# Hybrid encoder step on one core: stick-breaking attention written as a sum over running products times differences of neighbouring values

## The chip, the cores and the metric

The kernel runs on one core of one Trainium2 chip. The metric is the time of one execution in microseconds of the device. Before the change the median of three runs was 3561.26 us (3555.72 to 3566.15). Engines are named as in the profile: PE (TensorE matmul), PEld (its weight load), DVE (VectorE), ACT (ScalarE), POOL (GpSimd), SP (SyncE, which here only issues DMAs).

## The reference, cut to what matters

One layer: a norm, one wide projection, two mixers (stick-breaking attention with 8 heads of 64, and an RWKV recurrence with 8 heads), an output projection and a gated feed-forward layer, for a prompt of 2048 rows and a sample of 32 rows with 1024 cached keys. The change is in the attention of the prompt:

```python
z = jnp.einsum('bqhd,bkhd->bhqk', q, k) / math.sqrt(SB_HEAD_DIM)
mask = k_pos[None, :] < q_pos[:, None]
log_1mb = jnp.where(mask, jax.nn.log_sigmoid(-z), 0.0)
after = lax.cumsum(log_1mb, axis=3, reverse=True) - log_1mb
weight = jnp.where(mask, jnp.exp(jax.nn.log_sigmoid(z) + after), 0.0)
o = jnp.einsum('bhqk,bkhd->bqhd', weight, v)
```

So the weight of key s is sigmoid(z_s) times the product over all later keys j of (1 - sigmoid(z_j)). With R_s the product of sigmoid(-z_j) over all j from s on, that weight is R_(s+1) - R_s.

## The kernel before, in words

The program has three stages, and a scheduler that writes out one fixed order of instructions for each engine.

**Projection** (to about 911 us of the profiled execution). Three blocks of the prompt (5, 6 and 5 tiles of 128 rows); for each, 27 column groups of the projection in turn, each by three rounds of 8 matmuls (L323). The group of the attention's values is `g_va`, four times in each block: the columns are copied from PSUM to `vq`, and a deferred `fin` turns them on PE into rows (`tok_major`, L307, PSUM pool `psT` with 3 buffers), stores these, and splits them into a high and a low part `vs` (L656 on ACT, L657 on DVE) that are stored as `vhl_d`. `vs` lies in the tag `hl6`, of which there is one buffer; `qhl` of `g_qk` uses the same.

**Attention, recurrence and the first half of the output projection** (911 to about 1905 us). Three generators are interleaved by weights: `attention`, `recurrence` and `first_rows` (L738, `mo`). The attention goes over heads twice: first all 8 heads with the query groups 0 and 1 (512 queries each), here called the first half, then all 8 with the groups 2 and 3, the second half. For each group it goes down the key pieces `kc` of 512 keys, and for each piece over four tiles `j` of 128 queries; one such `scores` is a step. There are 96 steps in the first half (12 a head) and 224 in the second (28 a head); between heads 1 and 2 of the first half lies the sample's attention (6 steps). On the diagonal (`kc == qg`) a step has (j+1)*128 keys, else 512.

A step: two matmuls give `z` (L794, L795; PSUM pool `psZ`, 3 buffers), a third adds the mask on the diagonal (L797); `stick` then takes sigmoid(-z) to `R` (L754) and sigmoid(z) to `b` (L755) on ACT, DVE turns `R` into running products from the right (L757, a scan whose two operands are both `R`), and POOL multiplies `b` by the `R` of the next key (L758). Four steps later at the earliest `turn` transposes `b` on PE into `wt` (L809, `psW`, 2 buffers), and ACT and DVE split it into `wth` and `wtl` (L103, L104); two steps later `values` multiplies both parts with the values (L823, L824). `k` and `vp` are loaded at the first step that needs them (5 buffers each), `q` likewise.

**Feed-forward** (from about 2015 us): PE alone, L1268 and L1288.

Of the kernel before, what the change touches and what calls it, by code (L numbers as in the profile page):

```python
# [9 lines left out]
F32 = mybir.dt.float32  # L10
# [37 lines left out]
def f32(ap):  # L48
    return ap.bitcast(F32)
# [3 lines left out]
def kernel(ctx: ExitStack, tc: tile.TileContext, x_prompt, x_sample, cache_k, cache_v,  # L53
# [17 lines left out]
    vhl_d = [dp.tile([TP, 2, P], F32, name=f"vhl_d{c}") for c in range(4)]  # L71
    QR_d = dp.tile([NCH + 1, 4, P, P], F32, name="QR_d")
# [40 lines left out]
    with tc.tile_pool(name="pa0", bufs=1) as pe, tc.tile_pool(name="pa1", bufs=1) as pa, \  # L113
# [37 lines left out]
        R_MU, R_ST, R_W0, R_A0, R_KK, R_KA, R_RK = 0, 15, 30, 34, 38, 42, 46  # L151
# [110 lines left out]
        def superblock(sb, T0, NTILE):  # L262
# [478 lines left out]
    with tc.tile_pool(reuse_waits="tile", name="bp", bufs=6) as bp, \  # L741
# [8 lines left out]
        NB, LAG, LAG2, RW = 10, 4, 2, PAST + TS + 1  # L750

        def stick(z, R, b, k0, n):

# [8 lines left out]
        def queue(h):  # L762

            return ACT if h == 0 else SP

        def load(h, kc):
            k = bp.tile([P, 512], F32R, tag="k", name="k", bufs=5)
            queue(h).dma_start(f32(k), khl_d[h // 2][h % 2].rearrange("l d t -> (l d) t")[:, kc * 512:(kc + 1) * 512])
            v = bp.tile([P, 4, P], F32R, tag="vp", name="vp", bufs=5)
            queue(h).dma_start(f32(v), vhl_d[h // 2][kc * 512:(kc + 1) * 512, h % 2, :].rearrange("(j p) e -> p j e", p=P))  # L770
            pieces[h, kc] = [k, v]

        def scores(h, qg, kc, j):

            if kc == qg and j == 0:
                q = bp.tile([P, 2, 512], F32R, tag="q", name="q", bufs=3)
                cs = slice(qg * 512, (qg + 1) * 512)
                queue(h).dma_start(f32(q[:, 0]), qhl_d[h // 2][h % 2].rearrange("l d t -> (l d) t")[:, cs])
                for l in range(2):
                    queue(h).dma_start(f32(q[64 - 64 * l:128 - 64 * l, 1]), qhl_d[h // 2][h % 2, l, :, cs])  # L780
                state[h, qg] = q
            if j == 0 and (kc == qg or (qg == 2 and kc < 2)):
                load(h, kc)
            if kc == qg:
                R = bk.tile([P, RW], F32, tag="R", name="R")
                e = (qg % 2) * 512 + (j + 1) * P
                POOL.memset(R[:, e:e + 1], 1.0)
                state[h, qg, "R", j] = R
            R = state[h, qg, "R", j]
# [12 lines left out]
            state[h, qg, kc, j] = b  # L802
# [13 lines left out]
        def values(h, qg, kc, kb):  # L816
# [6 lines left out]
            PE.matmul(av[:, c0:], v[:, kb, :], wh[:, c0:], start=kc == qg and kb == 0, stop=False)  # L823
            PE.matmul(av[:, c0:], v[:, kb, :], wl[:, c0:], start=False, stop=kc == 0 and kb == 3)  # L824
# [7 lines left out]
        def s_scores(kc, e):  # L832
            n = TS if kc == 2 else 512
            if kc == 2:
                R = bk.tile([P, RW], F32, tag="R", name="Rs")
# [20 lines left out]
            b = bk.tile([P, 512], F32, tag="b", name="bs", bufs=NB)  # L856
            stick(z, state["R", e], b, kc * 512, n)
# [36 lines left out]
        def attention():  # L894
            A, B = [], []
            for hq, h in [(hq, h) for hq in range(2) for h in range(H)]:
# [7 lines left out]
                for qg in (2 * hq, 2 * hq + 1):  # L904
                    for kc in range(qg, -1, -1):
                        for j in range(4):
                            n = (j + 1) * P if kc == qg else 512
                            A.append((lambda h=h, qg=qg, kc=kc, j=j: scores(h, qg, kc, j), 2 * n / 2400))
# [446 lines left out]
```

## Time and profile before

| | |
|---|---|
| median of three runs | 3561.26 us |
| profiled execution, its time | 3553.88 us |
| its span, first to last instruction | 3551.9 us |
| PE, DVE, ACT, POOL busy over the span | 94%, 53%, 36%, 37% |
| granted TensorE clock, mean | 0.959 |

The span is 2 us shorter than the execution's time. A busy share is an average over the three stages, of which only the middle one is touched deeply by the change; it is read by stages below. A PE that is busy is not a PE at its peak, since the profile counts each matmul to its modelled end.

### The profile page before, as it was taken

To read this page: it belongs to the slowest core of one execution; us is meant where nothing else is said; L and a number is where in the kernel's file an instruction comes from. 1 tells how busy PE (TensorE), PEld (TensorE's weight loads), DVE (VectorE), ACT (ScalarE), POOL (GpSimd) and SP (SyncE) were. 2 spreads that over 40 slices of the span, in tenths; PEclk is the share of its full clock that TensorE was granted. 3 is DMA by queue.
4 is the path that set the end of the run, shared out by engine and by line. 5 is a ranking of instruction groups with operands and counts; after the bars stand their busy time and mean duration, and the time that the engine had idled before them with its cause. 6 is when DMAs were issued, how large, how long until landed. Compare 5 with 4: busy or idle time off the path is not lost.

```text
span 3551.9 us, 51561 instructions
## 1 busy us (share of the span) xinstructions
PE 3348.1 (94%) x20217; PEld 2888.5 (81%) x20217; DVE 1875.3 (53%) x2437; ACT 1265.8 (36%) x2419; POOL 1299.2 (37%) x1207
## 2 busy tenths in 40 slices
PE   8999999989788889998998999999999999999998
PEld 7988898879566677776777899989998888888887
DVE  4665757668876788988884332232222412212213
ACT  6444343443444566665563321111111311111111
POOL 3322433243444576657664322211221222122121
PEclk9999999999787899998999999999999999999999
DMA  5545655566644555554554341111111511111111
GB/s 150 162 145 152 201 147 151 181 172 182 198 117 114 133 148 142 150 139 127 154 138 137 118 132 48 48 36 48 48 48 36 167 60 48 48 48 48 48 42 48
DMA packets 480362, 395.81 MB, mean 111 GB/s; under 512 B 70820, under 2 KB 402160, under 8 KB 480120
## 3 DMA queue, kind: packets, MB, share of 16 engines
q1 hardware_dynamic: 391672, 346.51, 34.1%
q10 hardware_dynamic: 88448, 46.01, 4.8%
q8 instruction: 159, 2.61, 0.3%
q14 instruction: 83, 0.68, 0.1%
HBM read 278.16 MB, written 114.28 MB: 110 GB/s over the span
## 4 chain that ended last, share of the span: by engine, by line
PE 74%; DVE 14%; issue 4%; POOL 3%; ACT 2%; DMA 2%; SPq 0%; ACTq 0%; POOLq 0%; DVEq 0%
PE gu L1268 28%; PE dn L1288 14%; PE mm L323 12%; DVE R L757 5%; PE mo L738 4%; PE wt L809 2%; DVE wtl L104 2%; DVE t L541 1%; DVE Ti L543 1%; PE av L823 1%; PE a4ps L504 1%; PE av L824 1%; PE z L794 1%; PE sap L1067 1%; PE snp L1076 1%
## 5 line engine op out<-in xcount | busy, mean ns | idle before, releaser
L758 POOL TENSOR_TENSOR b<-b,R 128x512 f32<-128x512 f32 (+2 forms) x320 | 394.4, 1238 | 271.9 <-DVE R L757 174.1
L757 DVE TENSOR_TENSOR_SCAN R<-R 128x512 f32<-128x512 f32 (+2 forms) x320 | 440.9, 1387 | 40.0 <-ACT R L754 36.8
L1291 DVE TENSOR_TENSOR x<-x,dn 128x512 f32<-128x512 f32 x374 | 255.6, 687 | 243.4 <-PE dn L1288 243.4
L1268 PE MATMUL gu<-h2h,wh 128*128 128x352 f32 (+1 forms) x1760 | 368.3, 351 | 1.7 <-ACT wh L103 1.2
L1268 PE MATMUL gu<-h2h,wl 128*128 128x352 f32 (+1 forms) x1760 | 369.0, 351 | 0.0
L1268 PE MATMUL gu<-h2l,wh 128*128 128x352 f32 (+1 forms) x1760 | 367.3, 351 | 0.0
L1268 PEld LDWEIGHTS gu<-h2h,wh 128*128 128x128 f32 x1760 | 305.0, 188 | 33.9 <-ACT wh L103 1.4
L1268 PEld LDWEIGHTS gu<-h2l,wh 128*128 128x128 f32 x1760 | 305.3, 188 | 31.0
L1268 PEld LDWEIGHTS gu<-h2h,wl 128*128 128x128 f32 x1760 | 305.1, 188 | 30.2
L1288 PE MATMUL dn<-dh,hdh 128*128 128x512 f32 x748 | 295.1, 394 | 0.0
L1288 PE MATMUL dn<-dh,hdl 128*128 128x512 f32 x748 | 295.0, 394 | 0.0
L1288 PE MATMUL dn<-dl,hdh 128*128 128x512 f32 x748 | 293.8, 393 | 0.0
L809 PE MATMUL wt<-ident,b 128*128 128x128 f32 x1088 | 203.6, 300 | 87.5 <-DVE wtl L104 67.5
L809 PEld LDWEIGHTS wt<-ident,b 128*128 128x128 f32 x1088 | 137.2, 150 | 144.1 <-DVE wtl L104 68.9
L323 PE MATMUL mm<-hh,wh 128*128 128x384 f32 (+4 forms) x1296 | 248.2, 335 | 5.8 <-DVE qhl L614 2.0
L323 PE MATMUL mm<-hh,wl 128*128 128x384 f32 (+4 forms) x1296 | 234.6, 324 | 0.0
L323 PE MATMUL mm<-hl,wh 128*128 128x384 f32 (+4 forms) x1296 | 231.9, 321 | 0.0
L754 ACT ACTIVATE R<-z 128x512 f32<-128x512 f32 (+2 forms) x320 | 174.5, 545 | 142.3 <-PE z L795 69.2
L323 PEld LDWEIGHTS mm<-hh,wh 128*128 128x128 f32 (+1 forms) x1296 | 212.7, 194 | 13.1 <-DVE qhl L614 2.3
L103 ACT CAST wth<-wt 128x512 fp32r<-128x512 f32 (+1 forms) x320 | 169.7, 533 | 135.2 <-PE wt L809 124.7
L323 PEld LDWEIGHTS mm<-hh,wl 128*128 128x128 f32 (+1 forms) x1296 | 211.2, 190 | 2.6
L104 DVE TENSOR_TENSOR wtl<-wt,wth 128x512 fp32r<-128x512 f32 (+1 forms) x320 | 188.7, 595 | 41.3 <-ACT wth L103 38.4
(752 smaller groups left out, 5899.3 us busy)
## 6 DMA issues: line engine op xcount, KB each, us to landing
wraw<-in_w_in ACTq DMA_DIRECT2D x77, 512.0 KB
rawg<-in_w_gate SPq DMA_DIRECT2D x44, 512.0 KB
rawu<-in_w_up SPq DMA_DIRECT2D x44, 512.0 KB
rawd<-in_w_down SPq DMA_DIRECT2D x44, 512.0 KB
A_d<-a SPq DMA_DIRECT2D x28, 512.0 KB
mx<-mixT_d SPq DMA_DIRECT2D x27, 512.0 KB
k<-khl_d SPq DMA_DIRECT2D x42, 256.0 KB
vp<-vhl_d SPq DMA_DIRECT2D x42, 256.0 KB
```

Source lines behind the costliest of these rows:

```text
L103: ACT.copy(hi, src)
L104: (eng or DVE).tensor_tensor(lo, src, f32(hi), ALU.subtract)
L323: PE.matmul(ps[0:wd, 0:s1 - s0], a_[:, kt, 0:wd], b_[:, kt, s0:s1], start=i == 0, stop=i == 3 * KT - 1)
L504: PE.matmul(ps[:, j, :], KB[64 * e:64 * e + 64, j0 + j, :], QR[64 * e:64 * e + 64, j0 + j, :], start=True, stop=True)
L738: PE.matmul(ps[0:n], a_[:, kt, 0:n], b_[:, kt, :], start=j + kt == 0, stop=j == 2 and kt == KT - 1)
L754: ACT.activation(R[:, k0:k0 + n], z[:, 0:n], AF.Sigmoid, scale=-0.125)
L757: DVE.tensor_tensor_scan(rv, rv, rv, R[:, k0 + n:k0 + n + 1], ALU.mult, ALU.bypass)
L758: POOL.tensor_tensor(b[:, 0:n], b[:, 0:n], R[:, k0 + 1:k0 + n + 1], ALU.mult)
L809: PE.transpose(pt[:, j * P:(j + 1) * P], state[h, qg, kc, j][:, kb * P:(kb + 1) * P], ident)
L1268: PE.matmul(ps[:, 0:n], a_[:, kt, :], b_[:, kt, s0:s1], start=i == 0, stop=i == 23)
L1288: PE.matmul(ps[0:n], a_[:, i * P:i * P + n], b_[:, ds_], start=k == 0, stop=k == 3 * len(js) - 1)
L1291: DVE.tensor_tensor(x1[:n, ds_], x1[:n, ds_], ps[0:n], ALU.add)
```

## The change

It leaves `b` out. The sum over s of (R_(s+1) - R_s) v_s is summed by parts, to a sum of R_s (v_(s-1) - v_s). The differences `dv` are made in the projection (two subtractions on POOL for each `g_va`, the last column of the block before kept in spare columns of `cols`), transposed on PE (`pdv`), split into `vs` and stored as `vhl_d` in place of the values. On the diagonal, where R is 1 from the query on, the last row of each tile of 128 keys has to be v_(s-1) alone: these rows are stored as `ve_d`, and a diagonal block loads a second copy of its values, `vd`, with that row replaced. `values` on the diagonal therefore takes `vd` for the 128 queries of the tile, and `vp` for those after it: four matmuls instead of two, of as many columns together.

`stick` is one sigmoid and one scan. The scan's second operand, which the operation BYPASS ignores, is now `z` in PSUM instead of `R` in SBUF, and it starts from the first column of the piece to the right. `R` is a tile of its own for each step (12 buffers) and goes into `turn` in place of `b`. The sample's attention keeps the old form (`s_stick`). `load` is called up to 8 steps before the first step that needs it (`LOOK`), with 6 buffers for `k` and `vp`.

```diff
@@ g_va
+                dv = pr.tile([P, 2, MX], F32, tag="hl6", name="dv", bufs=1)[:, 0]
+                pv_ = cols[:, R_PV + c:R_PV + c + 1]
+                POOL.tensor_tensor(dv[:, 0:1], pv_, vq[:, 0:1], ALU.subtract)
+                POOL.tensor_tensor(dv[:, 1:NP], vq[:, 0:NP - 1], vq[:, 1:NP], ALU.subtract)
+                ACT.copy(pv_, vq[:, NP - 1:NP])
...
-                    vs = pr.tile([P, 6, 2, P], F32R, tag="hl6", name="vs", bufs=1)
-                    v4 = vt[:, 0:NTILE, :].rearrange("p j (h d) -> p j h d", d=HD)
-                    ACT.copy(vs[:, 0:NTILE, :, 0:64], v4)
-                    DVE.tensor_tensor(vs[:, 0:NTILE, :, 64:128], v4, f32(vs[:, 0:NTILE, :, 0:64]), ALU.subtract)
-                    SP.dma_start(vhl_d[c][T0:T0 + NP].rearrange("(j t) h e -> t j h e", t=P),
-                                 f32(vs[:, 0:NTILE]))
+                    for q0 in range(0, NTILE, 4):
+                        pt = psT.tile([P, 4, P], F32, tag="tr", name="pdv")
+                        m = min(q0 + 4, NTILE) - q0
+                        for i in range(m):
+                            PE.transpose(pt[:, i, :], dv[:, (q0 + i) * P:(q0 + i + 1) * P], ident)
+                        vs = r4("vs").bitcast(F32R).rearrange("p (j h e) -> p j h e", j=4, h=2)
+                        split(vs[:, 0:m, :, 0:64], vs[:, 0:m, :, 64:128],
+                              pt[:, 0:m, :].rearrange("p j (h d) -> p j h d", d=HD))
+                        t0 = T0 + q0 * P
+                        SP.dma_start(vhl_d[c][t0:t0 + m * P].rearrange("(j t) h e -> t j h e", t=P), f32(vs[:, 0:m]))
+
+                    pe_ = psT.tile([P, 512], F32, tag="tr", name="pve")
+                    PE.transpose(pe_[0:NTILE, 0:P], vq[:, 0:NP].rearrange("p (j t) -> p j t", t=P)[:, :, P - 2], ident)
+                    ve = pr.tile([P, 256], F32, tag="t2", name="ve").bitcast(F32R).rearrange("p (h e) -> p h e", h=2)
...
+                    SP.dma_start(ve_d[c, T0 // P:T0 // P + NTILE], f32(ve[0:NTILE]))
@@ attention
-        NB, LAG, LAG2, RW = 10, 4, 2, PAST + TS + 1
+        NB, LAG, LAG2, LOOK, RW = 12, 4, 2, 8, PAST + TS + 1
+        def stick(z, R, n, before):
+
+            ACT.activation(R[:, 0:n], z[:, 0:n], AF.Sigmoid, scale=-0.125)
+            rv = R[:, 0:n][:, ::-1]
+            DVE.tensor_tensor_scan(rv, rv, z[:, 0:n], before, ALU.mult, ALU.bypass)
...
+            k = bp.tile([P, 512], F32R, tag="k", name="k", bufs=6)
...
+            v = bp.tile([P, 4, P], F32R, tag="vp", name="vp", bufs=6)
+            dma(f32(v), src)
             if kc == qg:
...
+                vd = bp.tile([P, 4, P], F32R, tag="vd", name="vd", bufs=3)
+                dma(f32(vd[0:P - 1]), src[0:P - 1])
+                dma(f32(vd[P - 1:P]), ve_d[h // 2, 4 * qg:4 * qg + 4, h % 2, :].unsqueeze(0))
...
-            b = bk.tile([P, 512], F32, tag="b", name="b", bufs=NB)
-            if kc % 2 and kc < qg:
-                POOL.tensor_copy(R[:, 1024:1025], R[:, 0:1])
-            stick(z, R, b, (kc % 2) * 512, n)
+            R = bk.tile([P, 512], F32, tag="R", name="R", bufs=NB)
+            stick(z, R, n, 1.0 if kc == qg else state[h, qg, kc + 1, j][:, 0:1])
...
-            PE.matmul(av[:, c0:], v[:, kb, :], wh[:, c0:], start=kc == qg and kb == 0, stop=False)
-            PE.matmul(av[:, c0:], v[:, kb, :], wl[:, c0:], start=False, stop=kc == 0 and kb == 3)
+            if kc == qg:
+                vd = state[h, qg, "vd"]
+                for i, w_ in enumerate((wh, wl)):
+                    PE.matmul(av[:, c0:c0 + P], vd[:, kb, :], w_[:, c0:c0 + P], start=kb + i == 0,
+                              stop=qg == 0 and kb == 3 and i == 1)
+                c0 += P
+            if c0 < 512:
+                PE.matmul(av[:, c0:], v[:, kb, :], wh[:, c0:], start=False, stop=False)
+                PE.matmul(av[:, c0:], v[:, kb, :], wl[:, c0:], start=False, stop=kc == 0 and kb == 3)
...
+                while loads and loads[0][0] <= t + LOOK:
+                    load(*loads.pop(0)[1:])
```

The scheduler's order also moves. On PE, where one head of the first half ends and the next begins (between its 60th and 61st `z`, heads 4 and 5), there stood before, from the last `z` of the one head to the first of the next:

```order
L794 MATMUL z<-k,q 128x512
L795 MATMUL z<-k,q 128x512
L823 MATMUL av<-wth,vp 128x256
L809 MATMUL wt<-ident,b 128x128 x4
L824 MATMUL av<-wtl,vp 128x256
L823 MATMUL av<-wth,vp 128x128
L809 MATMUL wt<-ident,b 128x128 x3
...
L823 MATMUL av<-wth,vp 128x512
L824 MATMUL av<-wtl,vp 128x512
L794 MATMUL z<-k,q 128x128
```

The rows left out are more `wt`, `av` and rows of the recurrence; eight whole `turn`s stand between the two `z`. In the changed kernel the same place reads, on PE:

```order
L822 MATMUL z<-k,q 128x512
L823 MATMUL z<-k,q 128x512
L852 MATMUL av<-wth,vd 128x128
L852 MATMUL av<-wtl,vd 128x128
L856 MATMUL av<-wth,vp 128x384
L857 MATMUL av<-wtl,vp 128x384
...
L852 MATMUL av<-wth,vd 128x128
L822 MATMUL z<-k,q 128x128
L835 MATMUL wt<-ident,R 128x128 x4
L852 MATMUL av<-wtl,vd 128x128
```

The next head's first `z` now stands ahead of the first of those turns, and one turn then follows each `z`. At all seven boundaries between heads of the first half, five to nine turns stood between two `z`; in the changed kernel so many stand there at the sample's place (eight) and twice around the last head (five and eight), and elsewhere at most four.

The other place is on ACT, where the projection ends and the attention begins. Before, the loads of head 0 (ACT's queue issues them) stood among the last copies of the projection, the first of them 25 rows ahead of the first sigmoid:

```order
L778 DMA q<-qhl_d_57 128x512
L642 COPY vq<-mm 128x256
L780 DMA q<-qhl_d_57 64x512 x2
L768 DMA k<-khl_d_61 128x512
L770 DMA vp<-vhl_d_65 128x4x128
```

Now they stand behind all of it, on ACT, one after the other, right ahead of the first sigmoid:

```order
L104 CAST vs<-pdv 128x2x64
L796 DMA q<-qhl_d_57 128x512
L104 CAST ve<-pve 5x2x64
L798 DMA q<-qhl_d_57 64x512 x2
L803 DMA k<-khl_d_61 128x512
L808 DMA vp<-vhl_d_65 128x4x128
L812 DMA vd<-vhl_d_65 127x4x128
L813 DMA vd<-ve_d 1x4x128
...
L813 DMA vd<-ve_d 1x4x128
L772 ACT_TABLE_LOAD
L772 ACTIVATE R<-z 128x128
```

The rows left out are the same seven loads for the second query group: 14 issues in all, ten before.

## Rows read from the trace of the kernel before

**Rows 1.** The page: span and instructions; shares of the chain that ended last.

```profile
span 3551.9 us, 51561 instructions
PE 74%; DVE 14%; issue 4%; POOL 3%; ACT 2%; DMA 2%; SPq 0%; ACTq 0%; POOLq 0%; DVEq 0%
```

**Rows 2.** Both halves: PE, PEld, DVE, ACT, POOL busy; clock, DMA share, GB/s.

```profile
911.00:1206.00 295.00, 238.24 (x1648) 187.31 (x1649) 211.99 (x284) 146.47 (x337) 151.90 (x181) 0.77 0.50 132
1206.00:1878.00 672.00, 612.50 (x5065) 488.25 (x5065) 582.73 (x636) 407.04 (x818) 453.65 (x453) 0.95 0.53 140
```

**Rows 3.** Waits in the second half: total us, times, longest us.

```profile
POOL b L758 <- DVE R L757: 119.4, 86, 5.4
PEld wt L809 <- DVE wtl L104: 46.0, 37, 3.8
PE wt L809 <- DVE wtl L104: 42.9, 39, 3.7
```

**Rows 4.** Windows, matmuls of L794 alone, in six stretches of the first half.

```profile
962.00:987.00 25.00, 0.00 (x0) 0.00 (x0) 0.86 0.57 171
...
1098.00:1115.00 17.00, 0.00 (x0) 0.00 (x0) 0.70 0.44 122
1134.00:1151.00 17.00, 0.00 (x0) 0.00 (x0) 0.70 0.28 77
1167.00:1190.00 23.00, 0.00 (x0) 0.00 (x0) 0.55 0.44 127
sum 120.00, PE 0.00 PEld 0.00; mean PE 0.00 PEld 0.00
```

**Rows 5.** Windows, scans of L757 alone (DVE busy), first and second half.

```profile
911.00:1206.00 295.00, 117.97 (x100) 0.77 0.50 132
1206.00:1878.00 672.00, 327.30 (x225) 0.95 0.53 140
```

**Rows 6.** Groups by shape, 935 to 1910 us: busy us, mean ns.

```profile
L757 DVE TENSOR_TENSOR_SCAN R<-R 128x512 f32<-128x512 f32 x221 | 353.1, 1603 | 21.4 <-ACT R L754 19.3 <-POOL R L800 0.3
L104 DVE TENSOR_TENSOR wtl<-wt,wth 128x512 fp32r<-128x512 f32 x223 | 150.0, 677 | 35.2 <-ACT wth L103 33.1
L1083 DVE TENSOR_TENSOR VST<-VST,PC 64x512 f32<-64x512 f32 x31 | 35.7, 1151 | 1.0
L758 POOL TENSOR_TENSOR b<-b,R 128x512 f32<-128x512 f32 x223 | 294.6, 1326 | 176.5 <-DVE R L757 116.2 <-ACT b L755 17.7 <-ACT R L754 11.8
```

**Rows 7.** Timeline of DVE at the attention's first scans: start us, us.

```profile
921.30 0.47 DVE L757 TENSOR_TENSOR_SCAN R<-R 128x128 f32<-128x128 f32 x1
...
921.87 0.74 DVE L757 TENSOR_TENSOR_SCAN R<-R 128x256 f32<-128x256 f32 x1
...
922.69 1.01 DVE L757 TENSOR_TENSOR_SCAN R<-R 128x384 f32<-128x384 f32 x1
...
924.22 1.27 DVE L757 TENSOR_TENSOR_SCAN R<-R 128x512 f32<-128x512 f32 x1
```

**Rows 8.** Timeline, one step of the second half: matmul, sigmoid of `b`, scan.

```profile
1402.52 0.39 PE L795 MATMUL z<-k,q 128*128 128x512 f32 x1
...
1403.44 0.59 ACT L755 ACTIVATE b<-z 128x512 f32<-128x512 f32 x1
...
1403.77 1.26 DVE L757 TENSOR_TENSOR_SCAN R<-R 128x512 f32<-128x512 f32 x1
```

**Rows 9.** Timeline of the weight loads of two 128-column matmuls of `values`.

```profile
1408.07 0.19 PEld L823 LDWEIGHTS av<-wth,vp 128*128 128x128 f32 x1
...
1408.18 0.19 PEld L824 LDWEIGHTS av<-wtl,vp 128*128 128x128 f32 x1
```

**Rows 10.** The chain in order of time: one run of 512-column matmuls.

```profile
2085.86 24.97 PE dn L1288 x108
```

**Rows 11.** Timeline of PE in the projection: the transposes of one `tok_major`.

```profile
866.21 0.77 PE L307 MATMUL ptok<-ident,vq 128*128 128x128 f32 x5
```

**Rows 12.** Groups of POOL in the projection: busy us, mean ns.

```profile
L344 POOL TENSOR_TENSOR df<-xp 128x673 f32<-128x673 f32 (+5 forms) x45 | 65.4, 1453 | 196.3 <-ACT xp L335 123.6 <-ACT xp L337 50.4 <-ACT bon L486 18.2
```

**Rows 13.** Tile `q`: ACT's own issues of its loads, min/median/max ns.

```profile
L780 ACTq DMA_DIRECT2D q<-qhl_d x8: 452/603/978, 876.9 to 1247.1; - x8
```

**Rows 14.** Timeline of ACT at the first sigmoid.

```profile
917.58 0.28 ACT L754 ACTIVATE R<-z 128x128 f32<-128x128 f32 x1
```

More of the change, by code (lines that the diff above doesn't have):

```diff
@@ L71 @@
     vhl_d = [dp.tile([TP, 2, P], F32, name=f"vhl_d{c}") for c in range(4)]
+    ve_d = dp.tile([4, TP // P, 2, P], F32, name="ve_d")
     QR_d = dp.tile([NCH + 1, 4, P, P], F32, name="QR_d")
@@ L653, in fin @@
                         SP.dma_start(sv[:, c * P:(c + 1) * P], vt[0:TS, NTILE, :])
-                    vs = pr.tile([P, 6, 2, P], F32R, tag="hl6", name="vs", bufs=1)
-                    v4 = vt[:, 0:NTILE, :].rearrange("p j (h d) -> p j h d", d=HD)
-                    ACT.copy(vs[:, 0:NTILE, :, 0:64], v4)
-                    DVE.tensor_tensor(vs[:, 0:NTILE, :, 64:128], v4, f32(vs[:, 0:NTILE, :, 0:64]), ALU.subtract)
-                    SP.dma_start(vhl_d[c][T0:T0 + NP].rearrange("(j t) h e -> t j h e", t=P),
-                                 f32(vs[:, 0:NTILE]))
+                    for q0 in range(0, NTILE, 4):
[11 more added lines that the diff above has]
+                    ve = pr.tile([P, 256], F32, tag="t2", name="ve").bitcast(F32R).rearrange("p (h e) -> p h e", h=2)
+                    split(ve[0:NTILE, :, 0:64], ve[0:NTILE, :, 64:128],
+                          pe_[0:NTILE, 0:P].rearrange("p (h d) -> p h d", d=HD))
+                    SP.dma_start(ve_d[c, T0 // P:T0 // P + NTILE], f32(ve[0:NTILE]))
                 defer(1, fin)
@@ L764, in queue, with load @@
             return ACT if h == 0 else SP
[L766 to L775, printed above, removed]
+        def load(h, qg, kc):
+            dma = queue(h).dma_start
+            if kc == qg:
@@ L776, in scores @@
                 q = bp.tile([P, 2, 512], F32R, tag="q", name="q", bufs=3)
                 cs = slice(qg * 512, (qg + 1) * 512)
-                queue(h).dma_start(f32(q[:, 0]), qhl_d[h // 2][h % 2].rearrange("l d t -> (l d) t")[:, cs])
+                dma(f32(q[:, 0]), qhl_d[h // 2][h % 2].rearrange("l d t -> (l d) t")[:, cs])
                 for l in range(2):
-                    queue(h).dma_start(f32(q[64 - 64 * l:128 - 64 * l, 1]), qhl_d[h // 2][h % 2, l, :, cs])
+                    dma(f32(q[64 - 64 * l:128 - 64 * l, 1]), qhl_d[h // 2][h % 2, l, :, cs])
@@ L781, in scores @@
                 state[h, qg] = q
-            if j == 0 and (kc == qg or (qg == 2 and kc < 2)):
-                load(h, kc)
-            if kc == qg:
[L785 to L789, printed above, removed]
+            if kc < qg and not (qg == 2 and kc < 2):
+                return
+            k = bp.tile([P, 512], F32R, tag="k", name="k", bufs=6)
@@ new lines, in load @@
+            dma(f32(k), khl_d[h // 2][h % 2].rearrange("l d t -> (l d) t")[:, kc * 512:(kc + 1) * 512])
+            src = vhl_d[h // 2][kc * 512:(kc + 1) * 512, h % 2, :].rearrange("(j p) e -> p j e", p=P)
+            v = bp.tile([P, 4, P], F32R, tag="vp", name="vp", bufs=6)
+            dma(f32(v), src)
+            pieces[h, kc] = [k, v]
+            if kc == qg:
+                vd = bp.tile([P, 4, P], F32R, tag="vd", name="vd", bufs=3)
+                dma(f32(vd[0:P - 1]), src[0:P - 1])
+                dma(f32(vd[P - 1:P]), ve_d[h // 2, 4 * qg:4 * qg + 4, h % 2, :].unsqueeze(0))
+                state[h, qg, "vd"] = vd
@@ L790, in scores @@
+        def scores(h, qg, kc, j):
             k = pieces[h, kc][0]
@@ L834, in s_scores @@
             if kc == 2:
-                R = bk.tile([P, RW], F32, tag="R", name="Rs")
+                R = bs.tile([P, RW], F32, tag="Rs", name="Rs")
                 POOL.memset(R[:, PAST + TS:PAST + TS + 1], 1.0)
@@ L855, in s_scores @@
                           start=kc < 2, stop=True)
-            b = bk.tile([P, 512], F32, tag="b", name="bs", bufs=NB)
-            stick(z, state["R", e], b, kc * 512, n)
+            b = bs.tile([P, 512], F32, tag="bs", name="bs", bufs=4)
+            s_stick(z, state["R", e], b, kc * 512, n)
             state["b", kc, e] = b
@@ L894, in attention @@
         def attention():
-            A, B = [], []
+            A, B, loads = [], [], []
             for hq, h in [(hq, h) for hq in range(2) for h in range(H)]:
@@ L905, in attention @@
                     for kc in range(qg, -1, -1):
+                        loads.append((len(A), h, qg, kc))
                         for j in range(4):
```

7 lines of the change are left out of this document (4 added, 3 removed).

## The prediction

> **What bounds the kernel now.** I read the page first: PE makes up 74% of the chain that ended last, DVE 14% [rows 1]. The stages differ, so I went to the windows. Feed-forward and projection are PE's; the attention is not so simple, and its two halves have different limits [rows 2].
>
> In the second half (672 us) PE is busy for 612.5 us at a clock of 0.95, DVE for 582.7 us, 87%. Both are near full, and what ends PE's waits is DVE: before a transpose PE waits 42.9 us for `wtl` [rows 3], which reads the PSUM buffer the next `wt` needs. `wtl` is late because it queues behind a scan. POOL in turn waits 119.4 us for the scan [rows 3].
>
> In the first half (295 us) nothing is full: PE 81%, at a clock of 0.77, DVE 72% [rows 2]. The rows of `z` say why: six stretches of 17 to 25 us, 120 us together, hold not one `z` [rows 4]. Between heads the order lets the pipeline run empty: five to nine turns are worked off with no new sigmoid or scan behind them, then several `z` come at once and PE waits for them to get through ACT, DVE and POOL. In these stretches the granted clock is at its lower level for part of the time (0.55 to 0.86).
>
> Why are scans slow? A scan of 512 takes 1.27 us when POOL is not multiplying, and 1.01, 0.74 and 0.47 us for 384, 256 and 128 [rows 7]; the mean of the 221 of 512 is 1.603 us [rows 6]. The subtraction `wtl` of the same width, with one operand in PSUM, has a mean of 0.677 us amid the same POOL work, while the product L1083, half the partitions and both operands in SBUF, has 1.151 us [rows 6]. So DVE instructions that read two SBUF operands are held up by POOL, and POOL's product by them (1.326 us mean).
>
> **The change part by part.** All sums are against the profiled execution, 3553.9 us, which is 7.4 us below the median of 3561.3; its span is 3551.9 us.
>
> *Scans no longer held up, second half.* A head there has 22 scans of 512 and two each of the shorter three: 22 x 1.27 + 2 x 2.22 = 32.4 us, eight heads 259 us. They took 327.3 us [rows 5]: 68 us go. The change takes both causes away, the operand in SBUF and POOL's 224 products. The 31 L1083, at 0.68 us as the nearest row `wtl`, give 15 us over both halves; I put 12 here. DVE falls from 582.7 to about 503 us, 75% of the stretch.
>
> *PE there.* Its full-clock work is 612.5 x 0.95 = 582 us. The diagonal's split adds matmuls: 512 columns take 24.97 / 108 = 0.231 us [rows 10], a 128-column one starts 0.11 us after the one before [rows 9]. A pair of 128 and 384 then takes 0.11 + 0.17 = 0.28 instead of 0.23 us, 0.05 us more for each of 96 extra matmuls: 5 us. So 587 us of work stand in 672 us: 85 us are waits and low clock. Most of the waits with a name are for `wtl`, and a scan ahead of it will take 1.27 us instead of 1.6. I take 70% of the 85 us as gone: **-60 us**. Bounds: a quarter (-20, if waits for the recurrence and the loads come up in their place), and nearly all (-82).
>
> *First half.* The new order has one turn after each `z` at most boundaries, so the empty stretches go. What is left is DVE's work: 212.0 less the scans' excess. A head has 6 scans of 512 and two each of the shorter: 12.06 us, eight heads 96.5 us, and the sample's about 5.7 us, against 118.0 [rows 5]: 16 us; with L1083's share some 192 us remain. Run at 80%, between this half's 72% and the other's 87%, that is 240 us: **-55 us**. Bounds: 72% gives 267 (-28), 90% gives 213 (-82). PE's work here, 238 x 0.77 = 183 us, plus 5 us, fits if the clock does not stay low.
>
> *What goes off the path.* 320 sigmoids of `b` on ACT, POOL's products (294.6 us for those of 512 [rows 6]) and its copies of `R` lie beside PE and DVE. I cost them at nothing beyond the above: ACT is busy 50 to 61% and POOL 51 to 68% [rows 2].
>
> [...] A scan with one operand in PSUM is in no row. The nearest, `wtl`, reads PSUM and takes 0.677 us for 512 in the mean, which is no more than a DVE product of that width alone; so I leave the scan at 1.27 us. As an upper end I take the 1.603 us it has now, which would leave the second half only the gain from POOL's absence in the queue of waits, about -20 us. [...]
>
> *Projection.* Twelve `g_va` each get 5 or 6 more transposes and one for `ve`: 76. Five take 0.77 us with their tail [rows 11], about 0.12 us each: 9 us on PE, which is the chain there. Each `fin` now takes five buffers of `psT` instead of two, of three; a stall of about 0.5 us each, 6 us. POOL's two subtractions take 1.45 us as the like-sized L344 [rows 12], 12 times: 17 us, each beside the next group's 48 matmuls, so nothing, except that two-operand DVE work may wait as long. ACT and DVE split the same elements in two pieces instead of one, plus `ve`; small. In the last block `q` follows `va` directly and both use the one `hl6` buffer, so the copy of `q` on ACT now waits for the transposes of `dv`; other matmuls lie over it. **+15 us**, bounds +9 and +40.
>
> *Start of the attention.* Fourteen load issues stand on ACT in one run ahead of the first sigmoid. At 0.45 to 0.6 us each [rows 13] that is 7 us, of which the wait that already stood there (the first `z` stretch opens at 911, the first sigmoid starts at 917.58 [rows 14]) covers part: **+5 us**, bounds 0 and +12.
>
> *Loads.* 64 more for `vd`, a second read of 32 x 256 KB: 8 MB on top of some 133 MB of this stage (132 GB/s x 295 us and 140 x 672), at a DMA share of 0.50 to 0.53 [rows 2]; issued eight steps early, they are hidden. Should they not be, each of 32 blocks waits for a load.
>
> Sum: -60 - 55 + 15 + 5 = **-95 us**, 3553.9 - 95 = 3459 us.
>
> **The rivals.**
>
> *PE is already the bound.* PE's 91% in the second half speaks for it; against it, the profile counts matmuls to their ends, and 43 us of waits name DVE. Then the second half gives -20, the first -28 with the clock staying at 0.77, and the rest costs +20 to +30: 3525 to 3535 us.
>
> *More than forecast.* If both halves reach their upper bounds (-82 each) and the costs stay at +12: 3402 us. The evenness of the new order speaks for it; for the last tenths two engines in a fixed order would have to fit.
>
> *Slower: `z` is held until the scan is done.* `psZ` has three buffers. Before, one came free after ACT's `b`: in [rows 8] the matmul starts at 1402.52, `b` ends at 1404.03, the scan ends at 1405.03. Now the scan frees it, 1.0 us later here and more when DVE is behind. With three buffers and some 3 us a step (672 / 224) the hold decides once a scan ends more than about 9 us after its `z`, that is, when DVE is three steps behind; it is rarely so now. If every one of 320 steps lost 0.35 us, that is 112 us, the two gains of 115 us together would be eaten, and with +20 from projection and start the kernel would come to about 3571 us; with 0.4 us, 3587.
>
> *It does not do what it says.* The scan could stay at 1.6 us with its operand in PSUM. Then only the first half gains by its order: 3553.9 - 20 - 35 + 20 = about 3519 us.
>
> **How the numbers follow.** Chances: the forecast with its own range, 3400 to 3515 us, 0.70; below 3400, 0.07; PE bound or scan unchanged, 3515 to 3550, 0.11; no change, 0.04; slower, 0.08. I take 3400 to 3520 as the range. A difference of 0.3% (11 us) is about what a measurement of this kernel can tell from none. Faster by more than that 0.88, within it 0.04, slower 0.08.
>
> **What the changed profile would show.** Right: scans of 512 with a mean near 1.3 us and none over 2; no stretch over 12 us without a `z` at most boundaries of the first half, which takes about 240 us with a clock above 0.85; the second half about 612 us, DVE at about 82% of it, PE above 93%; the projection some 15 us longer and the first sigmoid about 20 us later than 917.6. Wrong: PE waiting for scans before `z` (more than 30 us in all); DVE over 90%; waits for `vd` or `k`; a projection longer by 40 us.

## The result, and the profile after

The changed kernel takes **3701.12 us** (median of four runs, 3697.21 to 3703.00) against 3563.70 us before (four runs; the 3561.26 further up are the first three of them): a ratio of 1.0387, 95% interval 1.0365 to 1.0408. It is slower by 3.9% where the forecast said 2.7% faster. The page of the changed kernel: span, then the shares of the chain that ended last, by engine and by line.

```profile
span 3695.4 us, 50876 instructions
...
PE 69%; DVE 10%; DMA 9%; SPq 4%; issue 3%; POOL 2%; ACTq 2%; ACT 2%; POOLq 0%; DVEq 0%
PE gu L1304 27%; PE dn L1324 14%; PE mm L324 9%; PE mo L756 5%; SPq L813 2%; PE wt L835 2%; DMA vd<-vhl_d 2%; ACTq L813 2%; DVE R L774 2%; DVE t L542 1%; DVE Ti L544 1%; PE z L822 1%; DMA mx<-mixT_d 1%; PE z L823 1%; PE snp L1112 1%
```

Beside [rows 1], three things are new on the chain: loads (DMA 9%, 2% before) and the queues of SP and ACT (none before), and the line is L813, the load of one row into `vd`. The windows of the two halves of the attention, cut at the first `z` of each and at the last, with the columns of [rows 2]:

```profile
959.00:1326.00 367.00, 242.57 (x1749) 198.98 (x1749) 171.89 (x252) 111.70 (x240) 22.57 (x25) 0.72 0.42 112
1326.00:2019.00 693.00, 627.30 (x5158) 506.82 (x5158) 495.58 (x634) 315.04 (x592) 125.51 (x100) 0.93 0.54 139
```

So of 143.5 us more in the span (3695.4 against 3551.9), 48 lie ahead of the first `z` (959 against 911), 72 in the first half (367 against 295), 21 in the second (693 against 672), 2 behind. DVE has no more work than was forecast (172 and 496 us, forecast 192 and 503), but PE stands still beside it. Now L813, min/median/max in ns:

```profile
L813 SPq DMA_DIRECT2D vd<-ve_d x28: 767/12644/24047, 977.1 to 1954.5; - x28
L813 ACTq DMA_DIRECT2D vd<-ve_d x4: 11197/17136/20479, 955.6 to 1334.4; - x4
```

One issue of 2 KB keeps its queue for 12.6 us in the median; [rows 13] has 0.6 us for `q`. Ahead of it on the same queue always stands L812, the load of 127 partitions. What that does to ACT, which issues head 0's loads, shows in its timeline (start us, us):

```profile
955.58 13.92 ACTq L813 DMA_DIRECT2D vd<-ve_d  x1
...
974.96 20.48 ACTq L813 DMA_DIRECT2D vd<-ve_d  x1
995.47 1.28 ACT L772 ACT_TABLE_LOAD   x1 [42.79 <-issue]
996.76 0.94 ACT L772 ACTIVATE R<-z 128x128 f32<-128x128 f32 x3
```

The first sigmoid is 79 us later than in [rows 14]; `z` was there at 959. And what moves meanwhile: the view of the DMA engines from 976 to 996 us, 40 slices, mean busy share of the 16 engines in tenths and GB/s.

```profile
DMA  8999940000000000000000000000000000000000
GB/s 267 311 319 350 272 115 27 22 22 22 23 22 22 20 22 20 20 20 22 20 20 20 22 20 20 20 22 20 20 20 20 22 20 20 20 22 20 20 20 22
```

After the spread loads, at 267 to 350 GB/s, two loads of `vd` are left, one on each queue, and together they get 20 to 22 GB/s. The window from 983 to 995 us has the share more finely (the last three columns: clock, DMA share, GB/s):

```profile
983.00:995.00 12.00, 0.00 (x0) 0.00 (x0) 0.00 (x0) 0.00 (x0) 0.00 (x0) 0.50 0.07 21
```

A share of 0.07 of 16 engines is the time of 1.1 engines (0.07 x 16): two loads on two queues together keep about one engine busy. 254 KB at 22 GB/s are 11.8 us (260,096 / 22,000); two that share the rate take 24 us, as the longest L813 does. PE, meanwhile, is busy for 2.36 of 42 us, and its granted clock is 0.50 (windows, same columns):

```profile
955.00:975.00 20.00, 2.36 (x9) 2.10 (x9) 0.00 (x0) 0.00 (x0) 0.00 (x0) 0.50 0.39 113
975.00:997.00 22.00, 0.00 (x0) 0.00 (x0) 0.00 (x0) 1.52 (x3) 0.00 (x0) 0.50 0.21 61
```

Two more views. PE's waits before `z` (total us, times, longest), and the scans of the attention by shape:

```profile
PE z L822 <- DVE R L774: 60.6, 15, 36.3
```

```profile
L774 DVE TENSOR_TENSOR_SCAN R<-R,z 128x512 f32<-128x512 f32 x224 | 283.0, 1265 | 56.0 <-ACT R L772 54.4
```

The scans are as forecast, 1.265 us against 1.603 in [rows 6], none over 1.29. The wait before `z` was one of the signs named against the forecast; behind the longest, 36.3 us, stands not a slow scan but a scan whose sigmoid stood behind issues on ACT.

### The profile page after: what moved, and what is told of

It reads as the page before. It is cut to its first block, busy times and chain, and to the rows that moved or that the text cites. A ratio compares the mean times of both kernels' runs of the same rounds, so it can differ in the third digit from the quotient of the medians.

```text
span 3695.4 us, 50876 instructions
## 1 busy us (share of the span) xinstructions
PE 3392.8 (92%) x20485; PEld 2938.9 (80%) x20485; DVE 1767.3 (48%) x2461; ACT 1145.2 (31%) x2135; POOL 858.9 (23%) x719
## 4 chain that ended last, share of the span: by engine, by line
PE 69%; DVE 10%; DMA 9%; SPq 4%; issue 3%; POOL 2%; ACTq 2%; ACT 2%; POOLq 0%; DVEq 0%
PE gu L1304 27%; PE dn L1324 14%; PE mm L324 9%; PE mo L756 5%; SPq L813 2%; PE wt L835 2%; DMA vd<-vhl_d 2%; ACTq L813 2%; DVE R L774 2%; DVE t L542 1%; DVE Ti L544 1%; PE z L822 1%; DMA mx<-mixT_d 1%; PE z L823 1%; PE snp L1112 1%
## 5 line engine op out<-in xcount | busy, mean ns | idle before, releaser
L774 DVE TENSOR_TENSOR_SCAN R<-R,z 128x512 f32<-128x512 f32 (+2 forms) x320 | 347.4, 1089 | 152.5 <-ACT R L772 150.0
L835 PE MATMUL wt<-ident,R 128*128 128x128 f32 x1088 | 195.5, 293 | 19.8 <-DVE wtl L105 19.0
L324 PEld LDWEIGHTS mm<-hl,wh 128*128 128x128 f32 (+1 forms) x1296 | 209.6, 188 | 2.6
L822 PE MATMUL z<-k,q 128*128 128x512 f32 (+2 forms) x320 | 139.5, 436 | 78.5 <-DVE R L774 60.6
```

What stands on the lines that cost most here:

```text
L324: PE.matmul(ps[0:wd, 0:s1 - s0], a_[:, kt, 0:wd], b_[:, kt, s0:s1], start=i == 0, stop=i == 3 * KT - 1)
L774: DVE.tensor_tensor_scan(rv, rv, z[:, 0:n], before, ALU.mult, ALU.bypass)
L822: PE.matmul(z[:, 0:n], state[h, qg][:, 0, js], k[:, 0:n], start=True, stop=False)
L835: PE.transpose(pt[:, j * P:(j + 1) * P], state[h, qg, kc, j][:, kb * P:(kb + 1) * P], ident)
```

## The experiments

Times are medians, each beside the kernel before on the same chip. The count of places where four or more turns stand between two `z` on PE comes from the written order; it is 15 before and 5 after. The kernel before took 3557.6 to 3561.5 us on these chips, so a difference between runs of two chips is good to some 4 us.

**First: is it the load of 127 partitions?** Theory A: the load of 127 partitions is not spread over the DMA engines, so that the next issue on its queue waits; B: the load of one row is slow; C: `z` is held too long. E1 cuts the load.

```diff
-                dma(f32(vd[0:P - 1]), src[0:P - 1])
+                dma(f32(vd[0:112]), src[0:112])
+                dma(f32(vd[112:P - 1]), src[112:P - 1])
```

> The changed kernel, with the load of 127 partitions into vd cut into one of 112 and one of 15. Theory A (the 127-partition load is not spread over the DMA engines; the trace shows about one packet of it at a time, some 41 a us, so 508 packets take about 12 us, and the next issue on the same queue waits for room): the issue of the one-row load after it falls from a median of 12.6 us to under 3 us (60 packets left in the odd part), and the kernel comes to 3440 to 3520 us. Theory B (a load of one partition in four pieces is itself slow to issue, whatever stands before it): that issue stays above 10 us and the kernel at about 3700 us. Theory C (the time is lost to PE waiting for scans before z, since z is held in PSUM): the issue times may change, the kernel stays within 30 us of 3700.

3551.06 us, ratio 0.9967 (0.9951 to 0.9983): 150 us gone by cutting one load in two. The one-row issue takes 0.63 us:

```profile
L814 SPq DMA_DIRECT2D vd<-ve_d x28: 612/625/659, 970.8 to 1805.1; - x28
```

The time is 31 us above theory A's range; what is left is taken up below. E2 swaps the two lines, the one row first.

```diff
-                dma(f32(vd[0:P - 1]), src[0:P - 1])
                 dma(f32(vd[P - 1:P]), ve_d[h // 2, 4 * qg:4 * qg + 4, h % 2, :].unsqueeze(0))
+                dma(f32(vd[0:P - 1]), src[0:P - 1])
```

> The changed kernel with the two loads of vd in the other order, the one row first. Theory A: the one-row load issues in under 1 us, and the issue that follows the 127-partition load (a load of q or k, or one of the recurrence) takes 10 to 20 us; the time stays at about 3700 us. Theory B: the one-row load still takes over 10 us, and what follows the 127-partition load is short.

One run, 3686.06 us. The one-row issue is short now (0.63 us) and the issues behind the 127 rows are long: 353 us in issues over 3 us in the whole execution, among them the store to `mixT_d`, `k`, `q` and the recurrence's loads. E3 puts both loads, into a tile that nothing reads, into the kernel before.

```diff
+                queue(h).dma_start(f32(vd[0:P - 1]), src[0:P - 1])
+                queue(h).dma_start(f32(vd[P - 1:P]), src[P - 1:P])
```

> The kernel before, with nothing but two loads added to each diagonal block: 127 partitions and one partition of its values into a tile that nothing reads. Theory A: the loads alone hold SP's queue for 32 times 12 us or more, and with it the recurrence's loads and the stores: 80 to 250 us slower than before. Theory C: since nothing waits for the tile and z is not held, within 30 us of before.

3764.58 us, ratio 1.0577 (1.0544 to 1.0610): 203 us from loads that no instruction uses. E4 takes the second copy away: `ve` holds the value of each tile's last key, and one matmul of that row with a row of ones corrects the sum on the diagonal.

```diff
...
+            PE.matmul(av[:, c0:], v[:, kb, :], wh[:, c0:], start=kc == qg and kb == 0, stop=False)
             if kc == qg:
+                PE.matmul(av[:, c0:c0 + P], state[h, qg, "vd"][:, kb, :], oner, start=False, stop=False)
...
+            PE.matmul(av[:, c0:], v[:, kb, :], wl[:, c0:], start=False, stop=kc == 0 and kb == 3)
```

> The changed kernel without vd: the diagonal uses vp like the rest, and one more matmul of one partition for each 128 keys adds the last key's value (ve_d holds that, 2 KB a block) times a row of ones; the rest of the change stays. Theory A: no issue on SP or ACT in the attention above 3 us, and the kernel at what was forecast for the change, 3430 to 3500 us. Theory C: 3650 us or more, with PE waiting over 100 us for scans before z.

3490.22 us, ratio 0.9814 (0.9786 to 0.9841). So the load of 127 is slow and holds the next issue on its queue, as A has it; B and C fall: the one row is fast by itself, and `z` is held as long here. Whether the held issues are what costs is asked below.

**Which counts are slow?** E8 and E11 are E1 with other cuts.

```diff
-                dma(f32(vd[0:112]), src[0:112])
+                dma(f32(vd[0:120]), src[0:120])    # E8; the rest is 7
+                dma(f32(vd[0:113]), src[0:113])    # E11; the rest is 14
```

> Kernel: the changed one, with the load of 127 partitions cut into 120 and 7 (the cut into 112 and 15 gave 3551 us, 127 uncut 3701). Theory M (only a count of partitions that is a multiple of 16 is spread over the DMA engines): the issues after the load of 120 are held up for 10 us and more as after 127, and the time is 3650 to 3700 us. [...]

> Kernel: the changed one, with the load of 127 partitions cut into 113 and 14. Theory D (a count of partitions with no divisor between 2 and 16 is not spread over the DMA engines, whatever it is): 113 behaves as 127, the issue after it takes 10 us and more in the median, and the time is 3660 to 3700 us. Theory S (127 alone is special, or what is small enough is spread anyway): the issue after it takes under 2 us and the time is 3540 to 3560 us.

E8 3547.97 us, ratio 0.9971 (0.9956 to 0.9986); E11 3700.69 us in one run. The issue behind the first load, in E8 (L813, the 7 rows), and in E11 (L813, the 14):

```profile
L813 SPq DMA_DIRECT2D vd<-vhl_d x28: 281/370/563, 974.1 to 1799.4; - x28
```

```profile
L813 SPq DMA_DIRECT2D vd<-vhl_d x28: 562/10964/19970, 976.7 to 1955.7; - x28
```

120 is no multiple of 16 and is fast (the issue behind it takes 0.37 us in the median), 113 is smaller and slow (10.96 us), so M and S fall: 113 and 127 are prime. In the counts tried, behind 127 and 113 the next issue takes 12.6 and 11.0 us, behind 120 and 112 0.37 and 0.50 us; 15, 14 and 7 are fast too, but carry little. Whether the divisors are the cause, and which other counts are slow, these runs don't show. For 127, the 1.1 engines' time above agrees with one engine; which engine it is, the traces don't show.

**Is it the wait on the queue, or the load?** E16 leaves the 127 rows whole and issues them from POOL's queue, which carries no other loads; E15 does the same with 120 and 7.

```diff
-                dma(f32(vd[0:120]), src[0:120])
-                dma(f32(vd[120:P - 1]), src[120:P - 1])
+                POOL.dma_start(f32(vd[0:120]), src[0:120])    # E15
+                POOL.dma_start(f32(vd[120:P - 1]), src[120:P - 1])
...
+                POOL.dma_start(f32(vd[0:P - 1]), src[0:P - 1])    # E16, for both
```

> Kernel: the changed one with the load of 127 partitions cut into 120 and 7 (3548 us), and these two issued by POOL's queue. All the rest is the change, the second copy is used. On PE four turns or more stand between two z at 2 places instead of 12. Theory R (what kept it 58 us above the row of ones is the order that the issues on SP and ACT brought): 3490 to 3505 us. Theory B (the bytes): 3540 us or more.

> Kernel: the changed one (3701 us) with the load of 127 partitions uncut, but issued by POOL's queue; the one row stays on SP's and ACT's. On PE four turns or more stand between two z at 2 places. Theory A (the load itself may be slow; the 240 us came from what stood behind it on its queue): no issue over 3 us is left on SP and ACT, and the time is 3465 to 3490 us. Theory G (the slow load delays av, wherever it is issued): PE waits for vd, and the time is 3550 us or more.

E15 **3468.95 us**, ratio 0.9750 (0.9724 to 0.9777); E16 3675.33 us, ratio 1.0322 (1.0291 to 1.0353). E15 is below both of its theories' ranges. Both have the same two places in the order. So theory A as E16 had it fails: with nothing queued behind it and hardly an issue held, the whole load still costs 206 us. From issue to landing (min/median/max us), E16 and E15:

```profile
DMA to landing us min/median/max: 20.4/24.7/32.2
```

```profile
DMA to landing us min/median/max: 2.8/4.4/8.0
```

The 206 us are not the price of the load on SP's queue: 24.7 us to landing are twice the 11.8 us worked out above, and one issue keeps POOL for 4.6 us (0.83 and 0.55 us for the two of E15). POOL itself is not the cause, since the waits of PE that name it come to 0.7 us. PE waits at a matmul of `vd` only once for long (11.5 us), so G fails too. What PE waits for in E16 is work fed by other loads, the recurrence (`mps`), `k` and the output projection (`mo`), though SP issued them in time (issues over 3 us make up 21 us in all). `issue` stands where the profile shows no releaser; `mps` reads nothing but two loaded tiles, `T` and `ABc`. The first four of PE's waits in E16, and what E15 has of the loads' lines:

```profile
PE mps L1049 <- issue: 42.6, 5, 14.9
PE z L822 <- DMA k<-khl_d: 37.5, 3, 27.9
PE mo L756 <- ACT mh L742: 27.9, 4, 10.5
PE mps L1049 <- DMA T<-Tinv_d: 21.7, 6, 7.7
```

```profile
PE z L823 <- DMA k<-khl_d: 14.6, 1, 14.6
...
PE mps L1050 <- DMA T<-Tinv_d: 1.7, 1, 1.7
```

The slow load makes loads of other queues late: the longest of these waits are 27.9 us for `k` and 7.7 us for `T`. That they share its one engine would explain it. The sizes of its packets in the trace fit: of the 1040 packets of a load in E16, 63 of 4 KB and one of 2 KB hold all its bytes, and 945 have 32 bytes, 15 for each of the 63; that one of the 16 engines has the data is an estimate from these counts and the 1.1 engines above. The records name no engine, so that the late loads wait for this one is argued, not shown.

**Why is the cut load still 79 us slower on SP and ACT (E8) than on POOL (E15)?** E10 is E4 with the change's four matmuls on the diagonal; E12 is E4 with the second copy loaded in 120 and 7 and not read; E13 has E12's loads with 32 numbers of a partition instead of 512; E14 has E12's loads on POOL's queue.

```diff
+                    PE.matmul(av[:, c0:c0 + P], v[:, kb, :], w_[:, c0:c0 + P], start=kb + i == 0, stop=False)    # E10
...
+                dma(f32(vd[1:121]), src[0:120])    # E12
+                dma(f32(vd[121:P]), src[120:P - 1])
...
+                dma(f32(vd[1:121, 0:1, 0:32]), src[0:120, 0:1, 0:32])    # E13
...
+                POOL.dma_start(f32(vd[1:121]), src[0:120])    # E14
```

> Kernel: the one with the row of ones (3490 us), with the diagonal's products cut into 128 columns and the rest, four matmuls a turn instead of two, as the change had them, and no second copy of the values loaded. Theory E (the cut costs what the forecast put it at, 96 short matmuls, 5 us): 3490 to 3500 us. Theory F (the 58 us between this kernel and the one with loads of 120 and 7 partitions are the matmuls): 3530 us or more.

> Kernel: the one with the row of ones (3490 us), with a second copy of each diagonal block's values loaded (120 and 7 partitions) that no matmul reads; the diagonal's products stay whole. On PE four to eight turns then stand between two z at 13 places instead of 2. Theory G (the 58 us between this kernel and the one with loads of 120 and 7 are the loads, with the order that their issues bring): 3535 to 3560 us. Theory E (a spread load is hidden, as forecast): 3490 to 3500 us.

> Kernel: the one with the row of ones and a second copy loaded that nothing reads (3597 us), with a sixty-fourth... of nothing else changed but the size: each of these loads carries 32 numbers of a partition instead of 512. As many loads are issued, and on PE four to eight turns stand between two z at 11 places (13 there, 2 without the loads). Theory R (the cost is the order, which the scheduler fills differently when more loads stand on the queues): 3550 to 3600 us. Theory B (it is the bytes, 8 MB more): 3490 to 3505 us.

> Kernel: the one with the row of ones and a second copy loaded that nothing reads (3597 us), with these loads of 120 and 7 partitions issued by POOL's queue instead of SP's and ACT's. The bytes are the same; on PE four turns or more stand between two z at 2 places instead of 13, as without the loads. Theory R (the cost is the order): 3488 to 3505 us. Theory B (it is the bytes and their DMA time): 3570 us or more.

| | time, us | ratio to before | places with 4 turns or more |
|---|---|---|---|
| E4 | 3490.22 | 0.9814 (0.9786 to 0.9841) | 2 |
| E10 | 3493.85 | 0.9810 (0.9791 to 0.9828) | 1 |
| E12 | 3596.57 | 1.0095 (1.0071 to 1.0119) | 13 |
| E13 | 3567.16 | 1.0029 (1.0013 to 1.0045) | 11 |
| E14 | 3499.17 | 0.9831 (0.9803 to 0.9860) | 2 |

The matmuls cost nothing that can be told. E12 is dearer than either theory had it. Without the bytes most of the cost stays (E13, 77 of 106 us); with the bytes, from POOL's queue and in the even order, it goes (E14, 9 us left). So it is not the bytes. E14 moves the queue and the order together, and PE's waits have to tell which it is; E4, then E13:

```profile
PE z L823 <- DMA k<-khl_d: 15.4, 2, 14.8
...
PE z L823 <- DVE R L774: 5.2, 8, 2.6
PE wt L836 <- DVE wtl L105: 5.0, 12, 1.7
```

```profile
PE wt L838 <- DVE wtl L105: 25.4, 39, 2.3
PE z L825 <- DVE R L774: 17.2, 18, 8.7
PE z L825 <- DMA k<-khl_d: 14.4, 1, 14.4
```

No load is later for PE; its waits for DVE are longer, by 32 us, and the clock of the first half is 0.78, where E10 has 0.90. That speaks for the order: the scheduler places PE's rows otherwise when more loads stand on SP's and ACT's queues, and bunches turns again. It is argued, not shown by an edit of the order alone, and the count of places does not measure the loss: E6 below has 15 and loses 26 us. Why the scheduler does so was not looked into.

**What the early loads and the scan's operand are worth.** E6 is E4 with `LOOK` 0; E7 is E4 with `R` in SBUF as the scan's unused operand; E17 is E10 with the same edit.

```diff
-        NB, LAG, LAG2, LOOK, RW = 12, 4, 2, 8, PAST + TS + 1
+        NB, LAG, LAG2, LOOK, RW = 12, 4, 2, 0, PAST + TS + 1
...
-            DVE.tensor_tensor_scan(rv, rv, z[:, 0:n], before, ALU.mult, ALU.bypass)
+            DVE.tensor_tensor_scan(rv, rv, rv, before, ALU.mult, ALU.bypass)
```

> Kernel: the one with the row of ones (3490 us), with loads issued at the step that needs them (LOOK 0 instead of 8). On PE, four to nine turns then stand between two z at 15 places again, as in the kernel before, instead of 2. Theory O (the first half's gain of 68 us is the order that early loads bring): the first half takes 275 to 300 us instead of 227, the second 630 to 650 instead of 628, and the time is 3540 to 3580 us. Theory W (it is the work that was taken away, the scans' excess, b and POOL's products): the first half stays under 245 us and the time within 15 us of 3490.

> Kernel: the one with the row of ones (3490 us), with R in SBUF again as the scan's unused second operand, in place of z in PSUM. Theory P (the scans of 512 fell from 1.60 to 1.27 us because POOL's products are gone): they keep a mean of 1.27 to 1.31 us, and the time stays within 8 us of 3490. Theory Q (the operand in PSUM did it): their mean goes to 1.4 us or more, which over 221 scans is 30 us of DVE or more, and the time to 3505 us or more.

> Kernel: the one with the row of ones and four matmuls (3494 us), with R in SBUF as the scan's unused second operand. On PE four turns or more stand between two z at 2 places (1 before the edit), so the order stays as even, unlike in the first try of this edit (8 places, 3553 us). Theory Q (the operand in SBUF costs by the scans that POOL holds up): the scans of 512 have a mean of 1.35 us or more, and the time is 3510 to 3550 us. Theory R (the first try was slow by its order): the time stays within 10 us of 3494.

E6 3516.31 us, ratio 0.9866 (0.9836 to 0.9895): between both theories. The first half takes 245 us, 18 more than E4's 227 and 50 less than before (295). So some 50 of the 68 us gained there do not need the early loads, with 15 places in the order as before. That the other 18 are the places is not shown: E10, with one place, takes 245 us there too, and 616 in the second half where E4 takes 629.

E7 3552.95 us, ratio 0.9990 (0.9969 to 1.0011), but with eight places in its order; E17, with two, 3541.58 us, ratio 0.9950 (0.9927 to 0.9972), 48 us above E10. Theory Q holds. Scans of E10, then E17, then one held scan of E17 and the POOL instruction beside it:

```profile
L774 DVE TENSOR_TENSOR_SCAN R<-R,z 128x512 f32<-128x512 f32 x224 | 283.8, 1267 | 68.7 <-ACT R L772 66.3
```

```profile
L774 DVE TENSOR_TENSOR_SCAN R<-R 128x512 f32<-128x512 f32 x224 | 315.0, 1406 | 58.1 <-ACT R L772 56.2
```

```profile
1402.76 2.90 DVE L774 TENSOR_TENSOR_SCAN R<-R 128x384 f32<-128x384 f32 x1 [3.31 <-ACT R L772]
```

```profile
1402.47 2.37 POOL L743 TENSOR_TENSOR mx<-mx,mh 128x1024 fp32r<-128x1024 f32 x1 [20.44 <-issue]
```

POOL's products are gone here, yet its other two-operand work holds a scan until it ends: 1404.84 - 1402.76 = 2.08 us, and 0.95 us for the scan itself (the mean of E10's 32 of 384), are 3.03 us against the 2.90 measured. With one operand in PSUM no scan is held (none over 1.29 us in the changed kernel). Nor is the scan itself dearer with it: 1.267 us with one operand in PSUM, 1.27 with both in SBUF and undisturbed [rows 7].

**The late first `z`.** E5 is E4 with `gv`'s product on DVE, `ve` in the unused half of `dv`'s tile and a `ve_d` for each pair of heads; E9 puts `dv` into a buffer of `r4` besides and `ve` into `vq`.

```diff
-                    POOL.tensor_tensor(vv, vv, gg, ALU.mult)    # E5
+                    DVE.tensor_tensor(vv, vv, gg, ALU.mult)
...
-                    ve = pr.tile([P, 256], F32, tag="t2", name="ve").bitcast(F32R).rearrange("p (h e) -> p h e", h=2)
+                    ve = dv2[:, 1, 0:256].bitcast(F32R).rearrange("p (h e) -> p h e", h=2)
...
-                dv2 = pr.tile([P, 2, MX], F32, tag="hl6", name="dv", bufs=1)    # E9
-                dv = dv2[:, 0]
+                dv = r4("dv")
```

> Kernel: the one with the row of ones (3490 us), and at the end of the projection three edits: POOL's product of gv goes to DVE, the rows ve get a buffer of their own and a store per pair of heads. Theory S (the 27 us that the first z is late beyond the projection's matmuls are a chain of queues: the subtraction dv stands behind gv on POOL, which waits for DVE, and ve waits for a buffer of the inverse): the first z comes at 940 to 950 us instead of 960, and the time is 3470 to 3482 us. Theory T (it is DVE's own work there, which any order must do first): the first z stays at 956 to 960 us, and the time within 5 us of 3490.

> Kernel: the one with the mended tail (3486 us, first z at 959.9), with the differences dv in a buffer of r4 instead of the single one of hl6, and ve in the finished columns vq. Theory H (the tail was the one buffer hl6: POOL waited 13.9 us for the store of qhl before it could write dv): dv runs by 932 us, the first z comes at 943 to 952 us, and the time is 3470 to 3482 us. Theory L (what counts is when the loads of head 0 land, which wait for the stores of the projection): the first z stays at 956 to 962 us and the time within 5 us of 3486.

In E4, `dv` stands on POOL behind `gv`, and `ve` on ACT waits for the buffer that it shares with the inverse (`t`); both rows, then the same place in E5:

```profile
936.72 1.75 POOL L596 TENSOR_TENSOR gv<-gv 128x512 f32<-128x512 f32 x1 [21.18 <-DVE gv L595]
```

```profile
952.95 0.25 ACT L104 CAST ve<-pve 5x128 fp32r<-5x128 f32 x1 [7.87 <-DVE Ti L544]
```

```profile
943.16 0.19 POOL L649 TENSOR_TENSOR dv<-pcols,vq 128x1 f32<-128x1 f32 x1 [13.86 <-DMA khl_d<-qhl]
```

E5 3486.25 us, ratio 0.9799 (0.9770 to 0.9827), not told apart from E4, with the first `z` at 959.9 as before the edit: the wait moved to the one buffer of `hl6`, which the store of `qhl` (here to `khl_d`) still reads. E9 brings the first `z` to 952.7 us, where PE has waited 21.8 us for the load of `k`, and yet takes 3501.78 us, ratio 0.9830 (0.9810 to 0.9850), since both halves take longer than E5's (238 and 643 us against 222 and 623); why was not looked into. Where the last 26 us go is shown in part; a kernel that wins them was not found.

## Why the prediction was wrong

*Loads: the step that failed.* "Issued eight steps early, they are hidden." The load was priced by its bytes (8 MB on 133) and by the early issue, and its shape was not looked at. 32 loads of 11.8 us are 378 us of loading at 22 GB/s. Uncut it costs 153 us on the change's own queues (against E8) and 206 us on POOL's (E16 against E15), with the same two places in the order. The sentence after it, "should they not be, each of 32 blocks waits for a load", named the case without a price, and no rival carried it. It also took the wrong waiter: not `av` for `vd`, but ACT and SP for the next issue, and in E16 the loads of others.

*The order, on the same term.* Also taken as free were 64 more issues on SP and ACT. With the load spread they cost 79 us on these two queues against POOL's (E8 against E15), most likely by the order.

*With both mended, the sum.* E15 is the change with the load cut and moved, and comes to 3469 us; the forecast was 3459. That it is so near is luck in part: the start costs 32 us more than forecast and the first half 13 less. Its windows and its span:

```profile
963.00:1190.00 227.00, 206.04 (x1739) 169.73 (x1739) 170.15 (x249) 110.64 (x239) 41.57 (x53) 0.91 0.70 177
1190.00:1801.00 611.00, 595.18 (x5164) 488.01 (x5165) 497.52 (x638) 312.48 (x592) 150.61 (x131) 0.98 0.61 159
```

```profile
span 3474.7 us, 51080 instructions
```

| term | forecast | E15, profiled | the change, profiled |
|---|---|---|---|
| projection and start | +20 | +52 | +48 |
| first half | -55 | -68 | +72 |
| second half | -60 | -61 | +21 |
| rest | 0 | 0 | +2 |
| sum | -95 | -77 | +143 |

*Projection and start: right in kind, too small.* The last projection matmul of E4 starts 22 us later than before (930.3 against 908.1; +15 with bounds +9 and +40). From there to the first `z` it takes 29 us instead of 3, where the forecast had 5 more and at most 12: it counted the issues and missed the queue behind `gv`, the shared buffers and the late loads.

*First half.* 227 us, 13 less than forecast, at a clock of 0.91. The number was near, the reason was not: the forecast gave all but 20 us of the gain to the order, and E6 keeps 50 of 68 us without the early loads. Most likely they came with the work that was taken off DVE, ACT and POOL, of which the forecast priced only DVE's; which part of it is not shown.

*Second half.* 611 us where 612 was forecast, PE busy 97% of it, DVE 81%.

*Scans.* 1.265 us where 1.27 was forecast; the rival in which they stay at 1.6 falls. Both causes were named; E17 shows that the operand is worth 48 us even with POOL's products gone.

*The rival with the right sign* held `z` until the scan. Its sign appeared (60.6 us of waits before `z`), its cause did not. E15 holds `z` as long, and PE waits there for scans no more than this:

```profile
PE z L823 <- DVE R L774: 5.4, 5, 3.4
```

In E17 `z` comes free after the sigmoid, and the kernel is slower than E10. The slower side had 0.08 for one mechanism; the one that happened was not among them. The rival "more than forecast" has costs of +12 where the sum has +20; with those it is 3410 us, not 3402, which changes nothing here.

## What to carry to other kernels

Look at the shape of every new DMA before its bytes: loads of 127 and of 113 partitions were slow here (the issue behind them took 12.6 and 11.0 us in the median), those of 120 and 112 were not (0.37 and 0.50 us), and 120 + 7 instead of 127 was worth 153 us. What is "issued early" still takes room in a queue and in a fixed order, so a transfer that is free in bytes can still cost (77 of 106 us stayed without the bytes), most likely by the rows that it displaces; a queue with nothing on it (POOL's, here) took the same loads 79 us cheaper. A page of waits names the engine that was late, not what its queue stood behind: read the queue's own rows first.

## What the runs showed of the hardware

In the changed kernel an issue behind the load of 127 held its whole queue, 12.6 us in the median and 24 us with two such loads at once, and ACT's arithmetic stood behind two of them for 34.4 of 42.8 us. Two such loads on two queues shared 20 to 22 GB/s. The same load made loads of other queues late with hardly an issue held (E16: 21 us of issues over 3 us, a wait of 27.9 us for `k`). A scan with both operands in SBUF was held by a POOL instruction on SBUF until that ended (E17: 2.90 us for 0.95), and none was with one operand in PSUM (none of 224 over 1.29 us in the changed kernel), though the scan ignores that operand.
